# Cross-covariance attention on Trainium2: the scaling of K^T Q moved to GpSimd and half a unit's work re-ordered

## The chip, the core and the metric

The kernel runs on one core of one Trainium2 chip. Five engines with instruction queues of their own work side by side: TensorE (PE in the profile, with its weight loads as PEld), VectorE (DVE), ScalarE (ACT), GpSimd (POOL) and SyncE (SP, which here only issues transfers). Each engine takes its instructions strictly in the order in which the program lists them, and waits at an instruction until the data that it needs has been produced. The metric is the device time of one execution in microseconds (us). Before the change it is 133.2 us, the median of six runs from 132.72 to 134.9.

## What is computed

Q, K and V are (8, 12, 512, 64) in float32. For each of the 96 heads:

```python
Q_norm = Q / (np.linalg.norm(Q, axis=-2, keepdims=True) + 1e-10)
K_norm = K / (np.linalg.norm(K, axis=-2, keepdims=True) + 1e-10)
attn = np.einsum('bhnd,bhne->bhde', Q_norm, K_norm)
attn = np.exp(attn - np.max(attn, axis=-1, keepdims=True))
attn = attn / (np.sum(attn, axis=-1, keepdims=True) + 1e-10)
return np.einsum('bhnd,bhde->bhne', V, attn)
```

The norms run over the 512 positions, so each head needs a 64x64 matrix of logits, a softmax over its rows, and V times that matrix.

## The kernel before

Four heads make a unit (`HU = 4`), so there are 24 units, 0 to 23. For each unit 512 KB of Q, of K and of V are loaded and 512 KB of output are stored: 96 transfers of 512 KB in all (the last store is cut in two). All of them are issued by SP, in the order in which the program lists them (L68 Q, L69 K, L73 V, L76 store).

What one unit goes through, by the names of the code:

- `cast_q` (L80) and `cast_k` (L83) on DVE turn Q and K into bfloat16, side by side in one tile of 128 columns per row.
- `grams` (L94): 64 small matmuls on PE build, for each head, the 128x128 product of [Q K] with itself, in PSUM (`gbuf`, a single buffer). Its diagonal holds the squared norms, its lower left block is K^T Q.
- `norms` (L106): four DVE instructions take the diagonals; then POOL raises them to the power -0.5 (L111, tile `rq`).
- `keep_kq` (L99): ACT copies the block K^T Q out of PSUM (tile `kq`).
- `scale_k` (L116): `kq` times `rq` of K, on 64 partitions x 256 elements (tile `kqs`).
- `logits` (L122): four PE transposes turn `kqs` into Q^T K, in PSUM (`lg`). `scale_q` (L126, DVE) multiplies by `rq` of Q, `exps` (L130, ACT) takes the exponential. No maximum is subtracted, since the logits are cosines.
- `normalise` (L134, L136, L138, DVE): sum over a row, reciprocal, product, written as bfloat16 into one of nine buffers (`abuf`).
- `doubled` (L152 on PE, L153 on ACT): a second copy of that matrix on the other 64 partitions, by way of `dup` in PSUM. `lg` and `dup` are two halves of one PSUM tile (`ltile`, shown as lgdup).
- V: `cast_v` (L87, ACT; DVE for the last four units), `vtrans` (L145 eight PE transposes, L147 an ACT copy out of PSUM), then `outs` (L163 matmuls, L167 two ACT copies, DVE sharing them at the end) and the store.

The order is written out by hand. The loop at L199 has one turn, a slot, per unit s. A slot lists, before the change: the loads of Q and K of unit s+3, V loads until `n1 + 3` units are loaded, the store of an older unit, then `cast_v`, `cast_q(s+1)`, `scale_k(s-1)`, `normalise(s-2)`, `grams(s)`, `norms(s)`, `cast_k(s+1)`, `doubled(s-2)`, `keep_kq(s)`, `outs` of one older unit, `logits(s-1)`, `scale_q(s-1)`, `exps(s-1)`, `vtrans`. Here `n1 = outs_by(s) = (s-2)*10//11`: outputs trail the loop, so that 5 of the 24 units (19 to 23) are still to be put out when the loop ends. `n1` is 17, 18 and 19 in slots 21, 22 and 23; slot 21 casts and transposes V of unit 17, slot 22 of unit 18, slot 23 of unit 19. Stores in the loop trail by four more units. Behind the loop (L236 on) the last unit's chain is finished, mixed with `outs` of the five units left, one after another.

In the following, "Q23" is the Q of unit 23, "V18" the V of unit 18, and "slot 22" the turn of the loop with s = 22.

Of the kernel before, what the change touches and what calls it, by code (L numbers as in the profile page):

```python
# [24 lines left out]
def kernel(  # L25
# [7 lines left out]
    nc = tc.nc  # L33
    B, H, N, _ = Q.shape
    assert N == NV * R and Q.shape[3] == D
    U = B * H // HU
# [5 lines left out]

    const = ctx.enter_context(tc.tile_pool(name="const", bufs=1))
    qp = ctx.enter_context(tc.tile_pool(name="qp", bufs=5))
    vp = ctx.enter_context(tc.tile_pool(name="vp", bufs=5))
    vbp = ctx.enter_context(tc.tile_pool(name="vbp", bufs=4))
    qkp = ctx.enter_context(tc.tile_pool(name="qkp", bufs=4))
    vtp = ctx.enter_context(tc.tile_pool(name="vtp", bufs=3))
# [9 lines left out]
    def outs_by(s):  # L58

        return max(0, (s - 2) * 10 // 11)  # L60
# [10 lines left out]
    def load_v(u):  # L71
        vf[u] = vp.tile([128, SV, TP * 2 * D], F32, name="vf")
        nc.sync.dma_start(out=vf[u], in_=Vf[u])  # L73

    def store(u, g=slice(0, SV)):
        nc.sync.dma_start(out=Of[u][:, g], in_=so[u][:, g].rearrange("p s t d -> p s (t d)"))  # L76
# [8 lines left out]
    def cast_v(u, copy=nc.scalar.copy):  # L85
        w = vb[u] = vbp.tile([128, SV, TP, 2 * D], BF16, name="vb")
        copy(w.rearrange("p s t d -> p s (t d)"), vf[u])  # L87
# [25 lines left out]
    def scale_k(u):  # L113

        kk = kqs[u] = small.tile([128, HU, D], F32, name="kqs")
        nc.vector.tensor_tensor(  # L116
            out=kk[D:], in0=kq[u][D:], in1=rq[u][D:, :, None].to_broadcast([D, HU, D]), op=ALU.mult,
        )

    def logits(u):  # L120
        for h in range(HU):
            nc.tensor.transpose(lg[:, h, :], kqs[u][D:, h, :], ident[D:, D:])  # L122
# [17 lines left out]
    def vtrans(u):  # L140

        ps = ps_v.tile([128, SV, TP, 128], BF16, name="vps")
        for g in range(SV):
            for t in range(TP):
                nc.tensor.transpose(ps[:, g, t, :], vb[u][:, g, t, :], identb)  # L145
        w = vt[u] = vtp.tile([128, SV, TP, 128], BF16, name="vt")
        nc.scalar.copy(w, ps)  # L147
# [7 lines left out]
    def outs(u, copies=(nc.scalar.copy, nc.scalar.copy)):  # L155
        s = so[u] = sop.tile([128, SV, TP, 2 * D], F32, name="so")
        a = abuf[u % len(abuf)]
        for g in range(SV):
            po = ps_o.tile([128, TP, 2 * D], F32, name="po")
            for t in range(TP):  # L160
                for x in range(2):
                    rows = slice(MV * x, MV * (x + 1))
                    nc.tensor.matmul(  # L163
                        po[rows, t, :], vt[u][:, g, t, rows],
                        a[:, 2 * g + x].rearrange("p a d -> p (a d)"), tile_position=(0, MV * x),
                    )
            copies[g](s[:, g], po)  # L167
# [22 lines left out]
    def on(f, u):  # L190
        if 0 <= u < U:
            f(u)
# [5 lines left out]
    nv, nst, nt = 2, 0, 0  # L198
    for s in range(U):  # L199
        n0, n1 = outs_by(s - 1), outs_by(s)  # L200
        on(load_qk, s + LOAD_AHEAD)
        while nv < min(U, n1 + 3):
            load_v(nv)
            nv += 1
        while nst < n1 - 3:
            store(nst)
            nst += 1
        new = range(nt, n1 + 1) if s >= 1 else ()
        for v in new:
            cast_v(v)  # L210
        on(cast_q, s + 1)
        on(scale_k, s - 1)
        on(normalise, s - 2)
        on(grams, s)
        on(norms, s)
        on(cast_k, s + 1)
        on(doubled, s - 2)
        on(keep_kq, s)
        for v in range(n0, n1):
            outs(v)  # L220
        on(logits, s - 1)
        on(scale_q, s - 1)
        on(exps, s - 1)
        for v in new:
            vtrans(v)
            nt = v + 1
# [8 lines left out]

    last = U - 1  # L236
    both = (nc.scalar.copy, nc.vector.tensor_copy)
    scale_k(last)
    logits(last)
    cast_v(n1 + 1, nc.vector.tensor_copy)  # L240
    normalise(last - 1)
# [49 lines left out]
```

## Time and profile before

| | before |
|---|---|
| median of six runs | 133.2 us (132.72 to 134.9) |
| the profiled execution, device time | 132.72 us |
| its span, first to last instruction | 130.9 us |
| mean granted TensorE clock | 0.78 |
| DVE busy | 100.5 us (77%) |
| ACT busy | 92.0 us (70%) |
| PE busy | 90.8 us (69%) |
| POOL busy | 42.6 us (33%) |
| bytes moved | 50.67 MB, mean 387 GB/s |

Lines of the profile's page name the source line, the engine, the operation and the tiles (out<-in), then the count, the busy time, the mean duration of one in ns, and the idle time of the engine just before such instructions with what ended it. Each of the 96 transfers has an issue time on SP and a time from issue to landing (median 10.2 us). The timeline lists instructions by their start, with the duration, so that a slot can be followed instruction by instruction; its clock is that of the span.

### The profile page before, as it was taken

The numbers are of one execution on the slowest core, as the hardware profiler recorded it, in microseconds if no ns is written. First come the engines' busy times: TensorE is split into PE (matmuls) and PEld (weight loads), VectorE is DVE, ScalarE is ACT, GpSimd is POOL, SyncE is SP. The second block draws the span as 40 slices with busy tenths as digits, with TensorE's granted clock in tenths as the row PEclk, the third lists the DMA queues.
The fourth block names the chain that finished last, engine by engine and source line by source line (L and its number), as shares of the span: only waits on it lengthen the run. The fifth ranks groups of instructions, "written<-read, shape, count | busy, mean of one in ns | idle before, by whom it ended". The sixth has DMA issues, their size and how long they took to land.

```text
span 130.9 us, 5371 instructions
## 1 busy us (share of the span) xinstructions
PE 90.8 (69%) x2232; PEld 71.0 (54%) x2232; DVE 100.5 (77%) x368; ACT 92.0 (70%) x161; POOL 42.6 (33%) x41
## 2 busy tenths in 40 slices
PE   0057753789679597838995498957889896677930
PEld 0046642668457375627773386845568675455730
DVE  0757878879999997949799998999987797682540
ACT  3003630568999999859887499899967879966560
POOL 7704540540444325404622445135521403300000
PEclk9999985555999959996589975799855559955595
DMA  4999999999999999999999999999999999999775
GB/s 139 392 417 397 401 407 412 402 400 400 402 397 412 400 422 399 410 404 407 405 411 406 416 404 410 411 405 412 402 413 405 415 399 403 404 406 351 293 273 217
DMA packets 20008, 50.67 MB, mean 387 GB/s; under 512 B 1552, under 2 KB 1552, under 8 KB 19984
## 3 DMA queue, kind: packets, MB, share of 16 engines
q1 hardware_dynamic: 19984, 50.34, 98.5%
q8 instruction: 17, 0.28, 0.8%
q14 instruction: 7, 0.06, 0.1%
HBM read 37.75 MB, written 12.58 MB: 384 GB/s over the span
## 4 chain that ended last, share of the span: by engine, by line
DMA 46%; DVE 19%; PE 13%; POOL 8%; issue 5%; ACT 4%; SPq 1%; POOLq 1%; ACTq 0%; DVEq 0%
DMA vf<-in_V_dram 23%; DMA qf<-in_Q_dram 18%; POOL rq L111 8%; DVE scr L106 5%; DMA kf<-in_K_dram 5%; PE vps L145 4%; PE gram L94 4%; DVE esum L134 3%; DVE ab L138 3%; PE po L163 3%; DVE kqs L116 3%; ACT vt L147 2%; DVE vb L87 2%; DVE rinv L136 1%; PE lgdup L122 1%
## 5 line engine op out<-in xcount | busy, mean ns | idle before, releaser
L111 POOL TENSOR_TENSOR rq<-nsq,mhalf 128x4 f32<-128x4 f32 x24 | 37.4, 1559 | 70.1 <-DVE nsq L106 70.1
L94 PE MATMUL gram<-qkb 32*128 32x128 bf16 x1536 | 37.7, 266 | 14.4 <-DVE qkb L83 9.4
L94 PEld LDWEIGHTS <-qkb 32*128 32x128 bf16 x1536 | 31.5, 119 | 18.7 <-DVE qkb L83 10.4
L147 ACT COPY vt<-vps 128x1024 bf16<-128x1024 bf16 x24 | 24.1, 1002 | 2.3 <-PE vps L145 2.0
L106 DVE CUSTOM_DVE_ANT_0 scr<-gram,ident 128x128 f32<-128x128 f32 x96 | 22.0, 281 | 4.3 <-PE gram L94 4.2
L167 ACT COPY so<-po 128x512 f32<-128x512 f32 x44 | 23.8, 588 | 0.9 <-PE po L163 0.4
L87 ACT CAST vb<-vf 128x1024 bf16<-128x1024 f32 x20 | 20.9, 1046 | 4.8 <-DMA vf<-in_V_dram 4.7
L80 DVE CAST qkb<-qf 128x1024 bf16<-128x1024 f32 x24 | 17.9, 746 | 5.7 <-DMA qf<-in_Q_dram 5.4
L163 PEld LDWEIGHTS <-vt 128*64 128x64 bf16 x384 | 15.5, 137 | 12.1 <-ACT vt L147 6.9
L163 PE MATMUL po<-ab,vt 128*64 128x128 bf16 x384 | 20.1, 264 | 1.3 <-DVE so L167 0.8
L145 PE MATMUL vps<-identb,vb 128*128 128x128 bf16 x192 | 19.0, 257 | 0.8 <-ACT vt L147 0.3
L152 PE MATMUL lgdup<-ab,identb 64*64 64x256 bf16 x24 | 8.0, 334 | 15.4 <-DVE ab L138 13.6
L145 PEld LDWEIGHTS <-vb 128*128 128x128 bf16 x192 | 14.2, 115 | 4.9 <-issue 1.6
L153 ACT CAST ab<-lgdup 64x256 bf16<-64x256 f32 x24 | 8.8, 368 | 11.0 <-PE lgdup L152 10.5
L83 DVE CAST qkb<-kf 128x1024 bf16<-128x1024 f32 x24 | 16.4, 683 | 0.0
L99 ACT COPY kq<-gram 64x256 f32<-64x256 f32 x24 | 8.8, 368 | 10.7 <-DVE nsq L106 10.3
L126 DVE TENSOR_TENSOR sl<-lgdup,rq 64x256 f32<-64x256 f32 x24 | 9.9, 414 | 6.4 <-PE lgdup L122 5.5
L122 PE MATMUL lgdup<-ident,kqs 64*64 64x64 f32 x96 | 11.5, 250 | 3.8 <-ACT ab L153 3.0
L130 ACT ACTIVATE ex<-sl 64x256 f32<-64x256 f32 x24 | 10.0, 418 | 4.3 <-DVE sl L126 4.1
L116 DVE TENSOR_TENSOR kqs<-kq,rq 64x256 f32<-64x256 f32 x24 | 10.1, 422 | 2.0 <-POOL rq L111 0.5
L122 PEld LDWEIGHTS lgdup<-ident,kqs 64*64 64x64 f32 x96 | 7.1, 123 | 8.1 <-ACT ab L153 5.6
L134 DVE TENSOR_REDUCE esum<-ex 64x4 f32<-64x256 f32 x24 | 9.9, 411 | 1.4 <-ACT ex L130 0.8
(16 smaller groups left out, 36.5 us busy)
## 6 DMA issues: line engine op xcount, KB each, us to landing
qf<-in_Q_dram SPq DMA_DIRECT2D x24, 512.0 KB, 10.2
kf<-in_K_dram SPq DMA_DIRECT2D x24, 512.0 KB, 10.2
vf<-in_V_dram SPq DMA_DIRECT2D x24, 512.0 KB, 10.2
out_dram<-so SPq DMA_DIRECT2D x23, 512.0 KB, 10.1
out_dram<-so SPq DMA_DIRECT2D x2, 256.0 KB, 2.6
```

The source lines that it names most:

```text
L80: nc.vector.tensor_copy(qkb[u][:, :, 0:D], qf[u])
L83: nc.vector.tensor_copy(qkb[u][:, :, D:], kf[u])
L87: copy(w.rearrange("p s t d -> p s (t d)"), vf[u])
L94: nc.tensor.matmul(gbuf[:, h, 0:2 * D], x, x, start=(t == 0), stop=(t == R - 1), tile_position=(NV * h, 0))
L106: nc.vector.tensor_tensor_reduce(out=scr, in0=gbuf[:, h, 0:2 * D], in1=ident, scale=1.0, scalar=1e-20, op0=ALU.mult, op1=ALU.add, accum_ou ...
L111: nc.gpsimd.tensor_tensor(out=r, in0=n2, in1=mhalf, op=ALU.pow)
L116: nc.vector.tensor_tensor(out=kk[D:], in0=kq[u][D:], in1=rq[u][D:, :, None].to_broadcast([D, HU, D]), op=ALU.mult,)
L122: nc.tensor.transpose(lg[:, h, :], kqs[u][D:, h, :], ident[D:, D:])
L145: nc.tensor.transpose(ps[:, g, t, :], vb[u][:, g, t, :], identb)
L147: nc.scalar.copy(w, ps)
L163: nc.tensor.matmul(po[rows, t, :], vt[u][:, g, t, rows], a[:, 2 * g + x].rearrange("p a d -> p (a d)"), tile_position=(0, MV * x),)
L167: copies[g](s[:, g], po)
```

## The change

Three things are edited. The product `scale_k` is issued on GpSimd instead of VectorE, and one slot sooner: for the unit s of the slot, right behind the power that GpSimd has just done, in place of unit s-1. In the slot, `logits`, `scale_q` and `exps` of unit s-1 come right behind it, ahead of `cast_k(s+1)` and `outs`, and `doubled(s-2)` comes behind `outs`; `keep_kq(s)` is now ahead of all of them. V is loaded one unit further ahead, with a sixth buffer. The call of `scale_k` for the last unit behind the loop falls away.

```diff
-    vp = ctx.enter_context(tc.tile_pool(name="vp", bufs=5))
+    vp = ctx.enter_context(tc.tile_pool(name="vp", bufs=6))
...
     def scale_k(u):
         kk = kqs[u] = small.tile([128, HU, D], F32, name="kqs")
-        nc.vector.tensor_tensor(
+        nc.gpsimd.tensor_tensor(
             out=kk[D:], in0=kq[u][D:], in1=rq[u][D:, :, None].to_broadcast([D, HU, D]), op=ALU.mult,
         )
...
-        while nv < min(U, n1 + 3):
+        while nv < min(U, n1 + 4):
             load_v(nv)
             nv += 1
...
         on(cast_q, s + 1)
-        on(scale_k, s - 1)
         on(normalise, s - 2)
         on(grams, s)
         on(norms, s)
-        on(cast_k, s + 1)
-        on(doubled, s - 2)
         on(keep_kq, s)
-        for v in range(n0, n1):
-            outs(v)
+        on(scale_k, s)
         on(logits, s - 1)
         on(scale_q, s - 1)
         on(exps, s - 1)
+        on(cast_k, s + 1)
+        for v in range(n0, n1):
+            outs(v)
+        on(doubled, s - 2)
...
     both = (nc.scalar.copy, nc.vector.tensor_copy)
-    scale_k(last)
     logits(last)
```

The order that each engine sees in a slot after the change: DVE `cast_q(s+1)`, `normalise(s-2)`, `norms(s)`, `scale_q(s-1)`, `cast_k(s+1)`; ACT `cast_v`, `keep_kq(s)`, `exps(s-1)`, two copies of `outs`, the copy of `doubled(s-2)`, the copy of `vtrans`; PE `grams(s)`, `logits(s-1)`, `outs`, `doubled(s-2)`, `vtrans`; POOL the power and `scale_k(s)`.

## The prediction, made before the changed kernel was run

> **What bounds the kernel now.** I read the 40 slices of the page first, then the windows, SP's issues, and the timeline of the last 30 us.
>
> ```profile
> DMA  4999999999999999999999999999999999999775
> GB/s 139 392 417 397 401 407 412 402 400 400 402 397 412 400 422 399 410 404 407 405 411 406 416 404 410 411 405 412 402 413 405 415 399 403 404 406 351 293 273 217
> ```
>
> The transfers run at about 405 GB/s from the second slice on and fall off only in the last four. The windows, whose columns are busy time of PE, PEld, DVE, ACT and POOL, then clock, DMA share and GB/s, say the same:
>
> ```profile
> 112.30:120.00 7.70, 5.08 (x54) 3.62 (x56) 4.98 (x12) 5.41 (x11) 1.01 (x1) 0.63 1.05 402
> 120.00:130.90 10.90, 5.31 (x80) 4.42 (x78) 3.37 (x5) 5.09 (x7) 0.00 (x0) 0.66 0.70 263
> ```
>
> Up to 120 us the queue is full; no reordering of compute shortens that part. In the last 10.9 us it has 0.70 of a full load: stores wait for outputs. So only the tail can give or take time, and the tail is set by when the last Q, K and V land and what compute still has to do then. SP's issues are one per 1.27 us, and landing is 10.2 us later:
>
> ```profile
> 91.57 0.38 SPq L73 DMA_DIRECT2D vf<-in_V_dram  x1
> 92.87 0.39 SPq L76 DMA_DIRECT2D out_dram<-so  x1
> 94.12 0.34 SPq L68 DMA_DIRECT2D qf<-in_Q_dram  x1
> 95.33 0.34 SPq L69 DMA_DIRECT2D kf<-in_K_dram  x1
> 96.62 0.38 SPq L73 DMA_DIRECT2D vf<-in_V_dram  x1
> ...
> 109.38 18.33 SPq L76 DMA_DIRECT2D out_dram<-so  x9
> ```
>
> These are V17, a store, Q23, K23, V18; from 109.38 SP has only stores left. The timeline shows who waits for them:
>
> ```profile
> 101.76 1.05 ACT L87 CAST vb<-vf 128x1024 bf16<-128x1024 f32 x1 [0.98 <-DMA vf<-in_V_dram]
> 104.33 0.67 DVE L80 CAST qkb<-qf 128x1024 bf16<-128x1024 f32 x1
> 106.81 1.04 ACT L87 CAST vb<-vf 128x1024 bf16<-128x1024 f32 x1 [0.86 <-DMA vf<-in_V_dram]
> 112.34 1.01 POOL L111 TENSOR_TENSOR rq<-nsq,mhalf 128x4 f32<-128x4 f32 x1 [3.21 <-DVE nsq L106]
> 115.87 0.42 ACT L130 ACTIVATE ex<-sl 64x256 f32<-64x256 f32 x1 [1.15 <-DVE sl L126]
> 117.14 1.01 ACT L147 COPY vt<-vps 128x1024 bf16<-128x1024 bf16 x1
> ```
>
> V17 and V18 are cast the moment they land (91.57 and 96.62 plus 10.2). Compute has caught up with the transfers; it is paced by them up to slot 22. Q23 (94.12 + 10.2 = 104.3) is cast just as it lands too. Earlier, slots without a wait take 3.98 us (`cast_k` at 71.71, 75.69, 79.67) with DVE without a gap, while four transfers take 5.1 us.
>
> **The change part by part.** All times below are on the clock of the profiled span, 130.9 us; its execution took 132.72 us, 0.5 below the median of 133.2, so a difference found on the span is added to the median.
>
> *V one unit deeper.* V3 is issued in slot 0 instead of slot 4, so every later Q and K moves back by one transfer: Q23 goes out where K23 did (95.33) and lands at 105.5, K23 at 106.8. V18 lands a slot sooner, and ACT's 0.98 and 0.86 us waits go. Late next is Q: `cast_q` is the first DVE instruction of a slot, and all of DVE's slot queues behind it. Price: +1.2 us on DVE in slot 22 (105.5 for 104.33). Stores shift by one place as well; the ones issued then were computed some 12 us before, so nothing waits.
>
> *The product off DVE.* It removes 0.45 us per slot (`kqs` at 73.40, the next at 73.85) from DVE's 3.98. Until compute catches up with the transfers this is worth nothing beyond that: ACT becomes the limit, its seven instructions pitch at 4.02 us (`cast_v` at 110.71, end of the V copy at 114.73), so slots stay near 4.0. From slot 3, where Q4 now lands at 21.2 (19.92 + 1.27), to slot 22 at 105.5 there are 19 slots of 4.44 us; the old kernel took 4.36 from slot 3 to slot 19, throttled slots and gaps included. So slot 22 should still be set by Q23.
>
> *Its price on POOL.* No row has this operation there. Below: POOL's one-input copy of 128 f32 took 0.29 us and its smallest instruction 0.10, so 256 elements take 0.10 + 2 x 0.19 = 0.48. Above: the longest power, 2.16 us. I take 0.86 (two inputs read one after the other, 0.10 + 4 x 0.19), which is nearest to the copy's row. The power's duration also shows how POOL and DVE collide: it takes 1.01 alone (112.34), but in dense slots it ends 0.04 us behind the Q cast (84.80 + 1.43 = 86.23 against 85.51 + 0.68 = 86.19; 63.16 + 2.16 = 65.32 against 65.28), while the casts never stretch (0.68 each). The product, behind the power, can lie over DVE's `ab` product (0.42). If DVE has to wait, up to 0.86 per slot, a slot of 3.53 + 0.86 = 4.39 is still under 4.44.
>
> [...]
>
> *The new order, slots 22 and 23.* DVE, by the pitches of the rows (cast 0.75 to the next, `normalise` 1.0, `norms` 0.87, `scale_q` 0.4, `cast_k` 0.68): Q23 at 105.5, `norms(22)` ends 108.1, `scale_q(21)` 108.5, `cast_k(23)` 109.2, `normalise(21)` 110.2. `grams(23)` from 109.2 takes 1.07 at full clock, `norms(23)` ends 111.4, the power starts by 111.7 (112.34 before). ACT: `exps(21)` is now queued ahead of the output copies and waits for `scale_q(21)` until 108.55; before, ACT ran without a gap from 106.81. Then exps 0.3, output copies 1.0, copy of `doubled` 0.3, V copy 1.0, and a slot of 4.02: the copy of V19 ends at 115.1, before at 114.73: **0.4 late.**
>
> *The tail.* Power until 113.0 (1.33, as where a cast covers its start), product until 113.9, `logits(23)` behind it. `logits` also waits for ACT's copy of `doubled` (8.6 us in 18 cases; both live in one PSUM tile), 114.1 here, so it ends near 114.6, `scale_q(23)` at 115.1, `exps(23)` at 115.6, **0.7 early** (116.29 before). DVE's `cast_v(20)` and `normalise(22)`, 1.6 us that lay between the last logits and `scale_q`, now lie beside power and product. But `outs(19)` needs the V19 copy: from 115.15 (114.78 before). Its 1.06 and `vtrans(20)`'s 1.04, at the half clock of 114 to 118 us, put the copy of V20 at 117.25, before 117.14; at full clock (0.64 and 0.62) ACT is free first at 116.75. From there the chain is unchanged: `doubled` twice, then rounds of 2.17 us. Sum: +0.1 to -0.4 us, I take -0.1: 133.2 - 0.1 = **133.1 us.** What the new order wins in the last unit, the later Q and ACT's queue take back.
>
> **The rivals.**
>
> *Faster.* The tail gains its 0.7 us or more whole: for it, the last softmax ends early, and PE may get the full clock in the tail, where a round would be ACT's 1.01 + 0.59 = 1.6 for 2.17; against it, ACT's queue. Its limit is the transfers: from 120 us on they have 0.70 x 10.9 / 1.04 = 7.3 us of work, done at 127.3 at the earliest, and by landings V23 comes at 118.3 and eight stores behind it at 1.27 each end at 128.5, against 127.2 + 2.6 = 129.8 for the last store now. So at most -1.3 to -1.5 us; priced at -1.2: **132.0 us.**
>
> *Slower.* The product on POOL is the late one in the last unit. ACT is free for `exps(23)` at 115.1; `scale_q(23)` ends at 114.25 plus the product's time, so from 0.85 us of product on, each us is a us of tail. At 2.16 us, +1.3 us, with 0.4 less if the rest of the tail was early: +1.0, **134.2 us.** In the loop it costs little: power, product and logits need 2.15 us plus the product between two units' norms, 4.3 at 2.16, under the 4.44 that transfers allow. For it: the power's 1.01 to 2.16 us; against it: the short copy row.
>
> [...]
>
> **How the numbers follow.** Forecast 0.42; faster 0.29; product late 0.18; DVE not relieved 0.11. About 0.5%, 0.67 us, is what a measurement of this kernel can tell from no change. The forecast's own range, -0.6 to +0.6, is within it; so faster 0.29, same 0.42, slower 0.29. The range takes -1.4 us of the faster rival, and +1.4 of the late product at its upper bound: 131.8 to 134.6. The forecast's own is 132.5 to 133.7.
>
> **What would show it.** GB/s still near 405 up to 118 us; DVE waits for Q (L80 <- DMA) in slots 20 to 22, ACT's for V gone; `cast_q(23)` at 105.5; ACT's L130 waits for L126 in those slots; `kqs` on POOL 0.5 to 1.6 us; the copy of V20 near 117.2, the last store issued near 127. Wrong would be: DVE never waiting for Q (then slots are slower than 4.44 and compute is late by itself), gaps in the transfers before 115 us, or a round of the tail of another length than 2.17 us.

## The result, and the profile after

The changed kernel takes 134.11 us (median of 29 runs, 133.16 to 134.92), the kernel before in the runs beside it 133.47 us (66 runs). The ratio is **1.0053, 95% interval 1.0037 to 1.0069**: slower by 0.5%, some 0.7 us. The forecast was 0.1 us faster. The time lies inside the whole range (131.8 to 134.6), but outside the forecast's own (132.5 to 133.7), and the sign was wrong. The profiled execution took 134.08 us with a span of 132.3 us (before 132.72 and 130.9). So this pair of profiles lies 1.4 us apart, twice the difference of the medians: lengths that are read from one pair carry that scatter, and the ratios of the experiments decide. Two experiments (V deeper alone, the copy beside `keep_kq`) have profiles from disturbed executions; these are not read here.

The page's transfer rows of the changed kernel, DMA share and GB/s in 40 slices:

```profile
DMA  4999999999999999999999999999999999998575
GB/s 160 357 390 408 397 403 409 403 401 398 405 399 401 407 414 402 414 401 410 407 409 401 412 412 407 407 412 410 404 416 403 413 398 409 401 403 323 219 263 218
```

As before, the queue is full up to some 118 us, and the difference is in the last four slices: 219 GB/s where the kernel before had 293. The windows (busy time of PE, PEld, DVE, ACT, POOL, then clock, DMA share, GB/s):

```profile
112.30:120.00 7.70, 4.47 (x54) 3.19 (x55) 4.42 (x11) 6.86 (x13) 2.26 (x2) 0.65 1.04 398
120.00:132.30 12.30, 6.21 (x89) 4.93 (x88) 3.37 (x5) 5.74 (x9) 0.00 (x0) 0.78 0.66 247
```

Between 112.3 and 120 us ACT is now busy for 6.86 of 7.70 us (5.41 before), though DVE is the engine that was relieved: over the span DVE fell from 100.5 to 89.5 us, and ACT rose from 92.0 to 96.0. The same 161 instructions take nearly as long as before if each is counted by itself (their durations add up to 100.1 us, before to 99.8): what grew is the time in which at least one of them runs, so they overlap less. SP's issues, Q23 first, then K23 and V19:

```profile
96.11 0.34 SPq L68 DMA_DIRECT2D qf<-in_Q_dram  x1
97.37 0.34 SPq L69 DMA_DIRECT2D kf<-in_K_dram  x1
98.68 0.38 SPq L73 DMA_DIRECT2D vf<-in_V_dram  x1
```

Q23 goes out 1.99 us later than before, not one transfer's 1.27. The timeline's instructions that answer to those shown of before:

```profile
106.46 0.69 DVE L80 CAST qkb<-qf 128x1024 bf16<-128x1024 f32 x1 [1.46 <-DMA qf<-in_Q_dram]
...
109.45 0.42 ACT L130 ACTIVATE ex<-sl 64x256 f32<-64x256 f32 x1
...
112.31 1.65 POOL L111 TENSOR_TENSOR rq<-nsq,mhalf 128x4 f32<-128x4 f32 x1 [0.85 <-DVE nsq L106]
...
114.04 0.61 POOL L116 TENSOR_TENSOR kqs<-kq,rq 64x256 f32<-64x256 f32 x1
...
115.30 0.37 ACT L153 CAST ab<-lgdup 64x256 bf16<-64x256 f32 x1
115.69 1.01 ACT L147 COPY vt<-vps 128x1024 bf16<-128x1024 bf16 x1
115.81 0.60 PE L122 MATMUL lgdup<-ident,kqs 64*64 64x64 f32 x4 [1.79 <-ACT ab L153]
...
117.00 0.42 ACT L130 ACTIVATE ex<-sl 64x256 f32<-64x256 f32 x1 [0.30 <-DVE sl L126]
...
118.89 1.01 ACT L147 COPY vt<-vps 128x1024 bf16<-128x1024 bf16 x1 [0.37 <-PE vps L145]
```

Line by line these are the cast of Q23, `exps(21)`, the power of unit 23, its product, the copy of `doubled(21)`, the copy of V19, `logits(23)`, `exps(23)` and the copy of V20. Read them as two chains. The logits' chain: the product is done at 114.65, but `logits(23)` starts at 115.81, when ACT's copy (until 115.67) has freed the shared PSUM tile. ACT's chain: from `exps(21)` at 109.45 ACT has no gap until the copy of V19 ends at 116.70; `outs(19)` and `vtrans(20)` follow, and the copy of V20 starts at 118.89. The forecast was 117.25; before it was 117.14. From there the tail is as it was: it ends at 128.42 with the last output copy (127.16 before).

The waits view (engine, line, what it waited for: us in total, times, longest) shows the same shift of the limits:

```profile
DVE scr L106 <- PE gram L94: 15.3, 15, 2.6
DVE qkb L80 <- DMA qf<-in_Q_dram: 10.4, 6, 4.0
...
PEld lgdup L122 <- POOL kqs L116: 8.3, 10, 1.1
...
PE lgdup L122 <- POOL kqs L116: 6.4, 10, 0.9
...
ACT vb L87 <- DMA vf<-in_V_dram: 2.5, 1, 2.5
```

DVE waits for Q 10.4 us (5.4 before) and for the grams 15.3 us (4.2 before); ACT's waits for V have fallen from 4.7 to 2.5 us. PE's gaps without a releaser have grown as well, from four with 4.9 us to nine with 9.3 us. They are not in the tail: the last one over 0.5 us ends at 102.60, and DVE waits another 1.46 us for Q23 after it.

### The profile page after: what moved, and what is told of

Its sections match the earlier page's. It is cut to its first block, busy times and chain, and to the rows that moved or that the text cites. A ratio compares the mean times of both kernels' runs of the same rounds, so it can differ in the third digit from the quotient of the medians.

```text
span 132.3 us, 5413 instructions
## 1 busy us (share of the span) xinstructions
PE 88.1 (67%) x2232; PEld 68.1 (52%) x2232; DVE 89.5 (68%) x344; ACT 96.0 (73%) x161; POOL 67.4 (51%) x65
## 4 chain that ended last, share of the span: by engine, by line
PE 23%; DMA 22%; ACT 21%; DVE 10%; issue 9%; POOL 9%; SPq 1%; ACTq 0%; POOLq 0%
DMA qf<-in_Q_dram 22%; ACT vt L147 8%; PE gram L94 7%; POOL rq L111 7%; PE vps L145 7%; PE po L163 5%; ACT so L167 5%; DVE scr L106 5%; ACT kq L99 3%; POOL kqs L116 2%; ACT ab L153 2%; PE lgdup L152 2%; PE lgdup L122 2%; ACT vb L87 2%; ACT ex L130 2%
## 5 line engine op out<-in xcount | busy, mean ns | idle before, releaser
L111 POOL TENSOR_TENSOR rq<-nsq,mhalf 128x4 f32<-128x4 f32 x24 | 46.4, 1934 | 43.8 <-DVE nsq L106 32.1
L94 PE MATMUL gram<-qkb 32*128 32x128 bf16 x1536 | 36.4, 259 | 16.7 <-DVE qkb L83 9.6
L94 PEld LDWEIGHTS <-qkb 32*128 32x128 bf16 x1536 | 30.4, 116 | 26.2 <-DVE qkb L83 15.5
L106 DVE CUSTOM_DVE_ANT_0 scr<-gram,ident 128x128 f32<-128x128 f32 x96 | 22.1, 284 | 15.4 <-PE gram L94 15.3
L80 DVE CAST qkb<-qf 128x1024 bf16<-128x1024 f32 x24 | 18.5, 772 | 10.4 <-DMA qf<-in_Q_dram 10.4
L163 PE MATMUL po<-ab,vt 128*64 128x128 bf16 x384 | 18.3, 245 | 2.7 <-issue 1.0
L163 PEld LDWEIGHTS <-vt 128*64 128x64 bf16 x384 | 13.8, 123 | 7.3 <-ACT vt L147 3.6
L116 POOL TENSOR_TENSOR kqs<-kq,rq 64x256 f32<-64x256 f32 x24 | 15.8, 657 | 2.8 <-POOL rq L111 1.1
L138 DVE TENSOR_TENSOR ab<-ex,rinv 64x256 bf16<-64x256 f32 x24 | 10.0, 418 | 0.8
## 6 DMA issues: line engine op xcount, KB each, us to landing
qf<-in_Q_dram SPq DMA_DIRECT2D x24, 512.0 KB, 10.4
```

The source lines that it names most:

```text
L80: nc.vector.tensor_copy(qkb[u][:, :, 0:D], qf[u])
L94: nc.tensor.matmul(gbuf[:, h, 0:2 * D], x, x, start=(t == 0), stop=(t == R - 1), tile_position=(NV * h, 0))
L106: nc.vector.tensor_tensor_reduce(out=scr, in0=gbuf[:, h, 0:2 * D], in1=ident, scale=1.0, scalar=1e-20, op0=ALU.mult, op1=ALU.add, accum_ou ...
L111: nc.gpsimd.tensor_tensor(out=r, in0=n2, in1=mhalf, op=ALU.pow)
L116: nc.gpsimd.tensor_tensor(out=kk[D:], in0=kq[u][D:], in1=rq[u][D:, :, None].to_broadcast([D, HU, D]), op=ALU.mult,)
L163: nc.tensor.matmul(po[rows, t, :], vt[u][:, g, t, rows], a[:, 2 * g + x].rearrange("p a d -> p (a d)"), tile_position=(0, MV * x),)
```

## The experiments

Ratios are to the kernel before, with 95% intervals; diffs are against the changed kernel unless it says otherwise. An interval is about 0.3% to each side, so single steps of 0.2% aren't told apart; 0.5% just is.

**1. V as deep as before.** `n1 + 4` becomes `n1 + 3`, the rest of the change stays.

> The changed kernel with V loaded as far ahead as before. Theory (the later Q sets the end): Q23 goes out and lands one transfer, 1.27 us, sooner than in the changed kernel, ACT waits for V17 and V18 again as before, and about 1 us of the loss is won back: some 0.8% faster than the changed kernel, 133.0 to 133.3 us where the kernel before has 133.5. Rival 1 (the new order on ACT and the shared tile lgdup make the last logits late, whatever Q does): it stays 0.5% slower than before, about 134.1, with logits of unit 23 still waiting for the copy of doubled. Rival 2 (the power and the product on GpSimd are late): the same 134.1, with logits waiting for the product.

Measured: 1.0018 [0.9984, 1.0052]. Q23 is cast at 104.22 (106.46) and the last power starts at 110.75 instead of 112.31. The timeline of this kernel:

```profile
112.65 0.61 POOL L116 TENSOR_TENSOR kqs<-kq,rq 64x256 f32<-64x256 f32 x1 [0.90 <-POOL rq L111]
...
114.60 0.60 PE L122 MATMUL lgdup<-ident,kqs 64*64 64x64 f32 x4 [1.79 <-ACT ab L153]
...
117.67 1.01 ACT L147 COPY vt<-vps 128x1024 bf16<-128x1024 bf16 x1 [0.37 <-PE vps L145]
```

Two thirds of the loss go with Q's delay (by the middle of the interval; it reaches from all to none). The product is done at 113.26, and the logits still wait until 114.60 for ACT: ACT is behind by itself.

**2. V deeper alone**, on the kernel before (`n1 + 4`, six buffers).

> The kernel before with V loaded one unit deeper and a sixth V buffer, and nothing else. Theory: it pays the later Q without the shorter chain on DVE: slot 22 starts 1.2 us later on DVE, but ACT's waits for V (0.98 and 0.86 us) go, so +0.2 to +1.0 us, 133.7 to 134.5. Rival 1 and 2 (order, or product): the same as before or a little faster, 133.0 to 133.5, since ACT's waits go and nothing else is touched.

Measured: 0.9998 [0.9962, 1.0034]. In the old order the later Q costs nothing that can be measured; it costs in the new one.

**3. The product alone**, on the kernel before: `scale_k(s)` on GpSimd behind `keep_kq(s)`, all else as it was.

```diff
-        on(scale_k, s - 1)
...
         on(keep_kq, s)
+        on(scale_k, s)
```

> The kernel before with the product on GpSimd behind the power, and neither the order of logits and doubled nor the loads of V changed. Theory: slots are paced by V and ACT, so little comes of it: -0.3 to +0.2 us, 133.2 to 133.7. Rival 2 (power stretched to 1.9 us and the product are late): slower, +0.5 us or more, with logits of the tail waiting for the product.

Measured: 1.0212 [1.0155, 1.0269]. The move by itself makes the kernel slower, by more than the whole change. In its waits DVE stands 12.5 us behind the grams (4.2 before) and 7.0 us behind the logits (5.5 before): PE still lists the logits behind `doubled` and the outputs. Its profile also has ten gaps of PE with no releaser, 13.4 us together, against four with 4.9 us before; what share of the 2.1% is theirs stays open.

**4. Q and K one unit deeper as well** (`LOAD_AHEAD = 4`, six buffers).

> The changed kernel with Q and K loaded four units ahead instead of three and a sixth buffer for each, so that the order of the queue between Q, K and V is that of the kernel before and all three are one unit deeper. Theory: Q23 lands about two transfers, 2.5 us, sooner than in the changed kernel, the loop's end comes sooner and the tail with it, down to the limit of the transfers: 132.0 to 132.8, faster than both. Rival 1 and 2: 133.8 to 134.2, the tail's own chain being unchanged.

Measured: 1.0027 [0.9991, 1.0063]. Q23 is cast at 104.89, 1.6 us sooner, but the last power starts only 0.2 us sooner (112.10), and the copy of V20 0.4 us (118.47). With Q there in time, compute is late by itself in this profile. So this cure of the late Q brings back 0.4 us at the copy of V20, where experiment 1 brought 1.2.

**5. `doubled` ahead of the outputs.**

```diff
+        on(doubled, s - 2)
         for v in range(n0, n1):
             outs(v)
-        on(doubled, s - 2)
```

> The changed kernel with doubled listed ahead of outs in the slot, so that its copy on ACT no longer sits behind the two output copies. Theory A (the wait of the last logits for that copy, through the shared tile lgdup, is what costs): logits of unit 23 starts about 1.1 us sooner (115.8 to 114.7 on the span's clock), the end follows, about 133.1 us. Theory B (ACT's queue as a whole is late in slot 23, 4.4 us of work whatever its order): logits starts sooner, but the copy of V19 and the outputs behind it don't, so the time stays, 133.9 to 134.3 us.

Measured: 1.0143 [1.0093, 1.0194]; no theory foresaw it. Its waits:

```profile
PE lgdup L152 <- DVE sl L126: 20.8, 22, 2.5
```

`doubled` doesn't write the shared tile before `scale_q` has read the logits in its other half. Now it waits for that in front of the outputs' matmuls, 20.8 us in 22 slots.

**6. The last V cast in the loop off ACT.** In slot 23 `cast_v` goes to DVE, behind `exps`.

```diff
         for v in new:
-            cast_v(v)
+            if s < U - 1:
+                cast_v(v)
...
         on(exps, s - 1)
+        if s == U - 1:
+            for v in new:
+                cast_v(v, nc.vector.tensor_copy)
```

> The changed kernel with the cast of V in slot 23 alone moved from ACT to DVE, behind scale_q, where DVE idled 1.1 us. Theory B (ACT's queue): ACT is 1.05 us shorter in slot 23, the copy of V19 ends at 115.7 instead of 116.7, all behind it follows, about -1.0 us: 133.1 us, 0.7% faster than the changed kernel and 0.2 to 0.4% faster than the one before. Theory A (the shared tile): logits of unit 23 comes sooner too, since the copy of doubled moves up with the rest, so the same; the two are told apart by the run with doubled ahead of outs. Theory C (the last Q): nothing changes, 134.1 us.

Measured: 1.0011 [0.9974, 1.0048]. One instruction of 1.05 us taken from ACT's last slot brings the copy of V19 from 115.69 to 114.36. Then another wait takes over, as its timeline shows:

```profile
111.94 2.25 POOL L111 TENSOR_TENSOR rq<-nsq,mhalf 128x4 f32<-128x4 f32 x1 [0.85 <-DVE nsq L106]
...
112.05 1.27 DVE L87 CAST vb<-vf 128x1024 bf16<-128x1024 f32 x2
...
114.93 0.41 PE L122 MATMUL lgdup<-ident,kqs 64*64 64x64 f32 x4 [1.45 <-POOL kqs L116]
```

Two casts in a row on DVE hold the power, which takes 1.01 us alone, for 2.25 us, and the logits now wait 1.45 us for the product.

**7. Both: V as before (1) and the last cast off ACT (6).**

> Both: V as far ahead as before the change, and the cast of V in slot 23 on DVE. If the later Q (theory C) and ACT's queue in the last slot (theory B) cost on top of each other, the last power starts near 110.8 (as with V not deeper) and the copy of V19 ends near 114.5: 132.2 to 132.8 us, faster than both kernels by about 0.7%. If one covers the other: 133.0 to 133.5.

Measured: 0.9974 [0.9938, 1.001]. The whole loss is gone; a gain over the kernel before isn't shown. The two casts again hold the power for 2.25 us (from 112.27) here.

**8. The new order and deeper V without GpSimd**: the product back on DVE, at its old place for unit s-1.

```diff
-        nc.gpsimd.tensor_tensor(
+        nc.vector.tensor_tensor(
...
+        on(scale_k, s - 1)
         on(normalise, s - 2)
...
-        on(scale_k, s)
```

> The changed kernel with the product back on DVE at its old place, for unit s-1 at the head of the slot: the new order and the deeper V without GpSimd. Theory D (the product on GpSimd costs more than it frees, as the run with that alone, 2.1% slower, suggests): faster than the changed kernel, 133.0 to 133.5. Theories B and C: DVE carries 0.45 us more per slot and the last unit's product comes a little sooner on DVE than on GpSimd (0.42 for 0.61); ACT's queue and Q are the same, so no gain: 134.0 to 134.6.

Measured: 1.0533 [1.0495, 1.0572], which no theory foresaw. Slots are a regular 4.80 us. One of them:

```profile
67.83 2.26 POOL L111 TENSOR_TENSOR rq<-nsq,mhalf 128x4 f32<-128x4 f32 x1 [2.54 <-DVE nsq L106]
67.95 0.67 DVE L83 CAST qkb<-kf 128x1024 bf16<-128x1024 f32 x1
...
68.55 0.68 DVE L80 CAST qkb<-qf 128x1024 bf16<-128x1024 f32 x1
...
70.13 0.42 DVE L116 TENSOR_TENSOR kqs<-kq,rq 64x256 f32<-64x256 f32 x1 [0.90 <-POOL rq L111]
```

In the new order `cast_k` of one slot and `cast_q` of the next stand side by side on DVE, right behind the power's start. The power ends at 70.09, 0.86 us behind the second cast, and DVE waits 0.90 us for it in front of the product. So the order needs the product on GpSimd and the product there needs the order: alone they cost 5.3% (with V) and 2.1%, together 0.5%.

**9 and 10. ACT's copy of `doubled` one slot later, beside `keep_kq`**, so that two instructions on the same partitions are neighbours on ACT again; in 10 with `cast_q` behind the normalise, V as before and the last casts moved as well.

```diff
         nc.tensor.matmul(dup[D:], identb[0:D, 0:D], a[0:D, :, 0, :], tile_position=(0, D))
-        nc.scalar.copy(a[D:, :, 1, :], dup[D:])
+    def doubled_copy(u):
+        nc.scalar.copy(abuf[u % len(abuf)][D:, :, 1, :], dup[D:])
...
+        on(doubled_copy, s - 3)
         on(keep_kq, s)
```

> The changed kernel with ACT's copy of doubled moved one slot on, right in front of keep_kq, which works on the same 64 upper partitions; PE's part of doubled stays. Theory B (ACT's order: seven instructions pitch at 4.30 us a slot in the changed kernel and at 3.9 before, because neighbours on other partitions don't overlap, and the copy of doubled stands in front of the last logits): a slot of ACT pitches at 4.0 to 4.1, logits of unit 23 no longer waits for the copy of doubled, the copy of V20 starts 0.7 us sooner, 133.3 to 133.6 us. Rival (the power, stretched by casts, and the later Q set the time): 133.9 to 134.3, with the pitch shorter and nothing following.

> The version that the runs so far point to: product on GpSimd and the new order as in the changed kernel, V not deeper, the cast of V of slot 23 on DVE, the copy of doubled beside keep_kq, cast_q behind normalise, and the cast of V20 behind normalise in the tail. If the causes add up: 132.0 to 132.6 us, 1% faster than the changed kernel and about 0.8% faster than the one before. If they cover one another: as with the first two alone, 133.2.

Measured: 1.0737 [1.0671, 1.0804] and 1.0522 [1.0477, 1.0567]. Both are misses. The waits of 10:

```profile
PE lgdup L122 <- ACT ab L155: 22.5, 18, 2.1
```

In its timeline the copy starts at 65.16, when the V cast ahead of it on ACT (64.10, 1.05 us) is over, and the logits start behind the copy, at 65.67. The exponential needs these logits (67.02), and ACT lists the output copies, the V copy and the next V cast behind it, so that the next copy comes at 70.40. The copy, put to the head of the slot, closes a loop: the logits wait for it 18 times through the shared tile. What ACT's neighbours cost could not be tried in this way.

**11. `cast_q` behind the normalise**, V still one deeper.

```diff
-        on(cast_q, s + 1)
         on(normalise, s - 2)
+        on(cast_q, s + 1)
         on(grams, s)
```

> [...] Theory E (the power's 2.25 us in dense slots, and the product behind it, hold logits, scale_q and with them cast_k): the power falls to 1.3 to 1.5 us, waits of logits for the product (14.7 us in all) mostly go, 133.2 to 133.6 us. Theory B (ACT): no more than 0.2 us gained, 133.9 to 134.2. Slower than 134.3 if normalise now waits for the exponential.

Measured: 0.9976 [0.9948, 1.0004], apart from the changed kernel's interval. Q23 comes as late as ever; what it holds up is less:

```profile
106.08 0.69 DVE L80 CAST qkb<-qf 128x1024 bf16<-128x1024 f32 x1 [1.25 <-DMA qf<-in_Q_dram]
...
110.95 1.01 POOL L111 TENSOR_TENSOR rq<-nsq,mhalf 128x4 f32<-128x4 f32 x1 [0.85 <-DVE nsq L106]
...
114.46 0.60 PE L122 MATMUL lgdup<-ident,kqs 64*64 64x64 f32 x4 [1.79 <-ACT ab L153]
...
117.53 1.01 ACT L147 COPY vt<-vps 128x1024 bf16<-128x1024 bf16 x1 [0.37 <-PE vps L145]
```

From the cast of Q23 to the last power it is 4.87 us; in the changed kernel 5.85. The power is shorter too (median 1.56 us, 2.05 in the changed kernel); experiment 12, which has that as well but Q in time, tells the two apart.

**12 and 13. The same with V as before**, and in 13 with the last casts moved too.

> The changed kernel with cast_q behind normalise and V as far ahead as before the change. If cast_q behind normalise gained 0.77% because Q is late and all of DVE queued behind it, then with Q on time it adds little to what V not deeper alone gave (1.0018 of the kernel before): 0.998 to 1.002. If it gained because it shortens the power on GpSimd, the gain adds up: 0.990 to 0.995, 132.0 to 132.7 us.

> The same with the cast of V in slot 23 on DVE and the cast of V20 behind normalise in the tail, so that no cast lies over the last power. ACT's last slot is 1.05 us shorter: 0.4 to 0.8% faster than the run without it. Together at best 0.988 of the kernel before, 131.7 us; 0.994 if the late Q was all that cast_q cured.

Measured: 1.0019 [0.9987, 1.0051] and 0.999 [0.9957, 1.0022]. With Q in time, the later `cast_q` adds nothing that can be measured to experiment 1 (1.0018). So what it cured was the late Q, and not the length of the power. In 13 two casts on DVE lie over the last power, which takes 2.50 us, and the logits wait 1.78 us for the product behind it.

**14. `cast_q` behind the normalise, and the last casts off ACT's path** (11 and 6, and in the tail `cast_v(20)` behind the normalise); V stays one deeper.

> After, with the normalise listed ahead of the Q cast, slot 23's V cast on VectorE, and V20's cast behind the normalise in the tail; V stays one unit deeper. If the late Q (0.96 us) and ACT's longer queue (0.7 us) are two causes that add: 1.0053 - 0.0077 - 0.0042 = 0.993 of before, the copy of V20 near 116.9 on the span, 2.0 us ahead of the changed kernel's 118.89. If both edits free the same wait, or the differences between the single cures were scatter: 0.997 to 0.999, the copy of V20 near 117.5 as with each alone.

Measured: 0.9983 [0.9957, 1.001]. In compute the two cures add in part: the copy of V20 starts at 116.32, 2.57 us sooner than in the changed kernel (0.84 of it an earlier Q23; 11 alone brought 1.36, 6 alone 1.69) and 0.8 sooner than before, and the last output copy ends at 125.97 (128.42; before 127.16). The time didn't follow. The windows of this kernel's tail, and the row of its last two stores (KB each, us from issue to landing):

```profile
120.00:126.00 6.00, 4.14 (x66) 3.46 (x64) 3.36 (x5) 4.29 (x7) 0.00 (x0) 0.77 0.86 330
126.00:131.00 5.00, 0.00 (x0) 0.00 (x0) 0.00 (x0) 0.00 (x0) 0.00 (x0) 0.52 0.52 195
```

```profile
out_dram<-so SPq DMA_DIRECT2D x2, 256.0 KB, 3.7
```

The last store is issued at 126.0, 1.3 us sooner than before (127.3), but lands at 129.8 (130.0 before). The span is 130.8 us, before 130.9. So in this profile the transfers, not compute, set the end. The mean of the second window hides how: the queue runs at its full share from 126.0 to about 128.5, so the last stores stand behind the others, and from 128.6 on there is only one chain of 2 KB packets, one every 0.08 us, until 129.5. That is about 25 GB/s, a sixteenth of the 400 of the full queue, so it looks like one of the 16 DMA engines a microsecond behind the rest. A packet of the instruction queue (16 KB, 0.98 us, at 117.48) may have put it there, since V23, in the queue at that time, landed 11.5 us after its issue where 10.2 is the median; this was not tested. Before, there is such a packet at 118.53 too, but the queue is nearly idle twice afterwards (DMA share 0.28 from 124.0 to 124.6, 0.36 from 126.0 to 126.5), and at the end it runs full until 129.5 (1.01 from 128.6 on). That compute can give no more isn't shown: up to 126 us the queue has 0.86 of a load that is 1.04 when full.

**15 and 16. `doubled` in a PSUM tile of its own**, taken from the pair of output buffers; in 16 with the edits of 14.

```diff
+        dup = ps_o.tile([128, TP, 2 * D], F32, name="po").rearrange("p t (x d) -> p (t x) d", d=D)[:, 0:HU]
         nc.tensor.matmul(dup[D:], identb[0:D, 0:D], a[0:D, :, 0, :], tile_position=(0, D))
```

> After, with the doubled product's PSUM tile taken from the pair of output buffers and not from the tile of the logits. Theory: in the changed kernel the logits of the last unit wait for the product from GpSimd nearly as long as for the copy of doubled (product ends 114.65, the logits start at 115.81 behind a copy that ends at 115.67), so 1.1 us of the tail go to the shared tile: the logits start near 114.7, the last exponentials at 115.9 for 117.00, the copy of V20 only 0.0 to 0.5 us sooner because ACT's own queue (outputs, doubled, V19) ends where it ended; ratio 1.001 to 1.005. Rival, the shared tile is the cause of the whole loss: copy of V20 at 117.6 or sooner, ratio 0.995 to 0.998. Second rival: doubled now waits for a free output buffer and hands that wait to the next outputs: ratio above 1.010.

> The two edits before in one kernel: Q cast behind the normalise, last casts moved, doubled in an output buffer. If late Q, ACT's queue and the shared tile are three separate costs: 0.988 to 0.992 of before, logits of the last unit started by their product near 113.2. If the shared tile costs nothing because ACT's queue ends the wait anyway: the same as the kernel without it, within 0.003.

Measured: 1.0653 [1.0609, 1.0697] and 1.0594 [1.0553, 1.0634]. The second rival of the first: `doubled` waits on PE for a buffer that ACT's output copies release, in a slot of 15 at 69.36, when the first copy (68.73 to 69.3) is over, and the transposes of V and the next grams stand behind it (the grams from 70.12 on):

```profile
68.73 1.07 ACT L168 COPY so<-po 128x512 f32<-128x512 f32 x2
...
69.36 0.27 PE L153 MATMUL po<-ab,identb 64*64 64x256 bf16 x1 [1.63 <-DVE qkb L80]
69.56 0.62 PE L145 MATMUL vps<-identb,vb 128*128 128x128 bf16 x8
```

The profile names the Q cast as releaser; that had begun at 68.66 and is of no tile that `doubled` uses, and the row that ends just before is the output copy. So what a free logits tile would be worth wasn't measured.

## Why the prediction was wrong

**"Only the tail can give or take time"** held. GB/s are about the same up to 118 us in both kernels, and the copy of V20 carries the loss: 1.64 us later than forecast in this profile. Two terms of the sum make that up. None of the signs that were named for being wrong came: DVE did wait for Q, the transfers had no gap before 115 us, and the rounds of the tail but the last kept their length. The slower rival was priced at 134.2 us, close to the measured 134.11, but that is luck: its mechanism, a late product, did not set the end.

**A term that was mis-sized: "Q23 goes out where K23 did (95.33) and lands at 105.5".** In the profile of the changed kernel it went out at 96.11 and was cast at 106.46, 0.96 us later. The mechanism, V3 ahead of Q4, was as put. Its size is known better than from this one pair: in the profiles of eight kernels with deeper V, Q23 goes out at 95.44 to 96.11, mean 95.74; in seven with V as before at 94.11 to 94.65, mean 94.33. So the edit costs 1.4 us, where 1.2 were forecast, and the changed kernel's profile shows the late end of that spread. From there the delay ran as described, `cast_q` ahead of all of DVE's slot: `exps(21)` at 109.45 for the forecast 108.55. What was wrong above all is that the new order would cover it: "what the new order wins in the last unit, the later Q and ACT's queue take back" left -0.1. Two edits that have only this delay in common, V as before (1) and `cast_q` one place later (11), bring the ratio to 1.0018 and 0.9976, and don't add (12). For 11 the interval lies apart from the changed kernel's, and 12 shows no such gain with Q in time, so that Q's delay at the head of DVE is a cause is shown. Its share is not known better than between 0.26% (Q and K deeper as well, 4) and 0.77% (11).

**The step that failed: "a slot of 4.02: the copy of V19 ends at 115.1".** I took ACT's pitch from the old order. From `exps(21)` to the end of the copy of V19 it was to be 6.55 us and was 7.25: the last slot, from its V cast on, took 4.41 us for 4.02 (112.29 to 116.70), and the part of the slot ahead of it 2.84 for 2.53. ACT's seven instructions, the old order first (the timeline of before), then the new:

```profile
106.81 1.04 ACT L87 CAST vb<-vf 128x1024 bf16<-128x1024 f32 x1 [0.86 <-DMA vf<-in_V_dram]
107.88 0.37 ACT L153 CAST ab<-lgdup 64x256 bf16<-64x256 f32 x1
108.15 0.37 ACT L99 COPY kq<-gram 64x256 f32<-64x256 f32 x1
108.54 1.07 ACT L167 COPY so<-po 128x512 f32<-128x512 f32 x2
109.50 0.42 ACT L130 ACTIVATE ex<-sl 64x256 f32<-64x256 f32 x1
109.82 1.00 ACT L147 COPY vt<-vps 128x1024 bf16<-128x1024 bf16 x1
110.71 1.05 ACT L87 CAST vb<-vf 128x1024 bf16<-128x1024 f32 x1
```

```profile
63.59 1.05 ACT L87 CAST vb<-vf 128x1024 bf16<-128x1024 f32 x1
64.73 0.37 ACT L99 COPY kq<-gram 64x256 f32<-64x256 f32 x1
65.12 0.42 ACT L130 ACTIVATE ex<-sl 64x256 f32<-64x256 f32 x1
65.57 1.07 ACT L167 COPY so<-po 128x512 f32<-128x512 f32 x2
66.66 0.37 ACT L153 CAST ab<-lgdup 64x256 bf16<-64x256 f32 x1
67.06 1.01 ACT L147 COPY vt<-vps 128x1024 bf16<-128x1024 bf16 x1
67.97 1.05 ACT L87 CAST vb<-vf 128x1024 bf16<-128x1024 f32 x1
```

Cast to cast it is 3.90 us before and 4.38 after, with the same durations (4.31 in the slots of the new order in which ACT waits for nothing). In the old order four neighbours overlap by about 0.1 us (108.15 starts before 107.88 + 0.37 = 108.25 is over); in the new order only the V copy and the next cast do. The two copies that a row with x2 holds overlap in both orders (1.07 us for two of 0.59).

The traces show which neighbours these are. `keep_kq` and the copy of `doubled` read and write on the partitions from 64 on, the other ACT instructions on those from 0 on. I counted, in the 16 profiles that are read here, the neighbours on ACT that follow each other within 0.06 us, so that hardly a wait lies between them, and compared each second one with the last ACT instruction that read from the same memory (SBUF or PSUM) and the last that wrote. Where one of the two worked on the other half of the partitions, none of 1270 overlaps; where both worked on the same half, 734 of 765 overlap by 0.05 us or more. This covers `exps` with the output copies behind it as well: both work from partition 0 on, but the last instruction that read PSUM ahead of these copies is `keep_kq`, from 64 on. In the old order two instructions of a slot follow such a change, in the new one five: three overlaps are lost. With the step of 0.02 to 0.03 us that stands in place of each, that makes the 0.4 us. It is a regularity of the traces and was not tested by an edit, since the two tries at neighbours (9, 10) brought in a loop of waits.

That ACT's queue is on the path is seen when an instruction is taken out of its last slot: the copy of V19 came 1.33 us sooner (6; 0.37 of it an earlier Q23), and with the other cure in place, 11 to 14, V20's copy moved from 117.53 to 116.32 (0.46 of it an earlier Q23). Of the queue's length, 0.4 us a slot are the pitch. In the measured time it is less clear: the edit brings 0.42% to the changed kernel (6) and 0.44% with V as before (7 against 1), each at the edge of the noise, and nothing where `cast_q` is later (14 against 11).

So of the 1.64 us, 0.96 are the cast of Q23, less 0.06 that `exps(21)` made up, and 0.70 ACT's pitch; PE's part between the two copies, at a granted clock of 0.50 (116.70 to 118.89), the half clock of the forecast, adds 0.04. With the mean issue times in place of this one profile's, the later Q is 0.2 us more than forecast and the pitch 0.7; the medians miss the forecast by 0.74 us (0.64 slower for 0.1 faster).

**"The product taken 0.86" on POOL.** It took 0.61 (median 0.61, mean 0.66; once 1.71, over casts). The row-based bounds held. "DVE not relieved", given 0.11, is excluded as what set the time: of the 48 casts of Q and K, 46 stayed at 0.67 to 0.70 us, and no run shows casts that wait as a rule for the product. Of the other two, the first cast of the program is long in both kernels (2.39 us, before 2.28), and the second shows that the product can hold a cast. It starts together with the product and ends 0.55 us behind it:

```profile
15.58 0.61 POOL L116 TENSOR_TENSOR kqs<-kq,rq 64x256 f32<-64x256 f32 x1
15.58 1.15 DVE L80 CAST qkb<-qf 128x1024 bf16<-128x1024 f32 x1 [0.96 <-DMA qf<-in_Q_dram]
```

The same is seen in 5, 6, 7, 12 and 14 (1.03 to 1.14 us, once in each).

**"Power 1.33 in the last unit."** It was 1.65, and in dense slots 2.25 (median 2.05, before 1.44), since the new order sets two casts in a row over it. That is the "product is late" rival by another instruction: not the product's own time but the power in front of it and, in 14, the product under a cast (1.37) made the logits wait, 1.45 to 1.78 us in 6, 7, 13 and 14. In the changed kernel's last unit it wasn't the end, since ACT came 1.0 us later still. Which of the two engines is held goes both ways: in the two rows at 15.58 it is the cast, until the product is nearly done (1.15 us for 0.68); in the last unit the power starts 0.11 us ahead of the V cast on DVE (112.42, 0.68 us) and is the one that is held (1.65 us for 1.01). What decides it isn't shown.

**"`logits` also waits for ACT's copy of `doubled`, 114.1 here"** was right as a mechanism: PE stands 1.79 us in the changed kernel and in 1 and 11, in the changed kernel 1.0 of it after the product is done. In the changed kernel it doesn't set the end, by the order of ACT's queue: even with logits at 114.7 the copy of V19 would end at 116.70 and `outs(19)` start behind it. No run shows that by itself.

**The faster rival's floor, "-1.3 to -1.5 us",** was not reached and isn't refuted. I counted eight stores at 1.27 us each behind V23, which end at 128.5. In 14 compute ended 1.2 us sooner than before, and nearly all data had moved by 128.5; the last packets, one after another, took until 129.5, and the span was 0.1 us shorter. What the floor left out, as far as these packets show, is one DMA engine that is behind the others. This is one profile; over its runs the kernel of 14 is 0.2% faster than the one before, within noise. Whether that is why no version beat the kernel before isn't shown, for 7 and 13 in particular.

**Rounds of 2.17 us** in the tail held (121.77 to 123.94), and the last one took 1.76 us at a higher clock (0.76 granted from 123.94 to 125.70, 0.50 in the round before).

What stays open: the late Q costs in the new order and not in the old one (2); how much of the 2.1% of experiment 3 is PE's unexplained gaps; and why the last packets of 14 came so late.

## What to carry to other kernels

A pitch read from one order of an engine's queue belongs to that order (ACT's, cast to cast: 3.90 us in the old, 4.38 in the new): when instructions are re-ordered, count them pair by pair, look which half of the partitions each works on, and leave some room in the sum. A load that moved ahead of another in a full queue (Q23 issued 1.4 us later) was paid here by the engine at whose head the later one stands, in the new order though not in the old (2, 0.9998), so first look at what is queued behind that instruction; listing it one place later (11, 0.77%) was worth more here, by the middle of the intervals, than loading Q and K earlier as well (4, 0.26%). And before tuning compute in a tail, find when the last transfer could end with compute out of the way, and then look at the packets too: in the one profile in which compute was 1.2 us ahead (14), the end came 0.1 us sooner.

## What the runs showed of the hardware

- ACT instructions overlap their neighbours by about 0.1 us in some orders and not in others (3.90 against 4.31 us for the same seven, without waits). Of 1270 that read or wrote on the other half of the partitions (from 0 or from 64 on) than the last ACT instruction that read the same memory or that wrote, in 16 profiles, none overlapped its neighbour; of 765 others 734 did. The old order has two of the first kind in a slot, the new one five.
- A power of four elements per partition takes 1.01 us on GpSimd by itself, 1.65 with one DVE cast (0.68) in its time and 2.25 with two in a row; it then ends 0.86 us behind the last cast (8: 70.09 against 69.23), in other slots 0.04 (before: 65.32 against 65.28). It is held about as long as the casts run (0.64 us more with one, 1.24 with two), and they stay at 0.67 to 0.70 under it. With the product of 0.61 us it goes both ways: it was held by casts (1.71 in the changed kernel, 1.37 in 14), and it held a cast that started with it or just behind it (1.15 for 0.68 us).
- Two halves of one PSUM tile are waited for as one: `logits` for the copy out of `dup` (1.79 us in the changed kernel's last unit, 22.5 us in 18 waits in 10), and `doubled` for the read of `lg` (20.8 us in 22 waits when it came first).
- What waits at the head of an engine's queue holds what is listed behind it: in 5 `doubled` stood those 20.8 us with the outputs' matmuls behind it. In the profiles of both kernels PE's 2232 matmuls ran in the listed order, and so did the units' instructions on ACT, DVE and POOL.
